# A hybrid S5 and attention layer on one core: x loaded first, parameters on GpSimdE's queue, C in longer runs, warm-up products ahead, another order of steps

## The chip, the cores and the metric

The kernel runs on one core of one Trainium2 chip, as one program. The metric is the device time in microseconds. TensorE multiplies and transposes into PSUM, VectorE and ScalarE work on SBUF and PSUM, GpSimdE works on SBUF, and loads are issued from the queues of SyncE, ScalarE and GpSimdE and carried by 16 DMA engines.

## The reference

One decoder layer on x of 256 tokens by 1024, all in float32. After an RMS norm, one projection (1024 to 2048) gives S5 inputs u and attention q, k, v. The S5 part has 32 groups of 16 channels with a diagonal complex state of 64 each; attention has 8 heads of 64 and, with 256 tokens, one causal block. Both outputs are normed, projected, added to x; then comes a SwiGLU layer of 2816.

```python
h = rmsnorm(x, g_pre_mix)
z = jnp.einsum('bsd,de->bse', h, w_in)
u, q, k, v = jnp.split(z, [D_SSM, D_SSM + D_ATTN, D_SSM + 2 * D_ATTN], axis=-1)
...
dt = jnp.exp(log_dt.astype(f32))[:, None]
mag = jnp.exp(a_re * dt)
ang = a_im * dt
lb_re = mag * jnp.cos(ang)
lb_im = mag * jnp.sin(ang)
...
bu_re = jnp.einsum('bsgh,gph->bsgp', uf, bb_re)
...
y = (jnp.einsum('bsgp,ghp->bsgh', st_re, c_re.astype(f32))
     - jnp.einsum('bsgp,ghp->bsgh', st_im, c_im.astype(f32))
     + d_skip.astype(f32) * uf)
...
mix = jnp.concatenate([rmsnorm(y_ssm, g_ssm_out), rmsnorm(y_attn, g_attn_out)], axis=-1)
x = x + rmsnorm(jnp.einsum('bse,ed->bsd', mix, w_out), g_post_mix)
h = rmsnorm(x, g_pre_ffn)
f = jax.nn.silu(jnp.einsum('bsd,df->bsf', h, w_gate)) * jnp.einsum('bsd,df->bsf', h, w_up)
x = x + rmsnorm(jnp.einsum('bsf,fd->bsd', f, w_down), g_post_ffn)
```

## The kernel before

The 256 tokens are two tiles of 128 partitions (`x_sb[0]`, `x_sb[1]`, four loads each). TensorE transposes x (L529), ScalarE and VectorE scale it by the gain into `xf`, and the four parts of the input projection multiply `xf` with weights that arrive in halves of pieces (`raw`, 512 KB each, L202): u (L564), then q and k (`qk_ps`, L873), then v (L899). All weight halves go out on SyncE's queue; a buffer must be free before its next load is issued, and the queue is served in order.

Beside that runs the S5 preparation. The parameters (`ldt`, `par_a`, `par_b`) are loaded, transposed on TensorE (L496, L497) and copied out of PSUM by VectorE into `par` (L498). From `par` VectorE computes the step by an exact exponential (`exp_a`, `exp_m`, `exp_k`, `exp_e`, `exp_r`, all 128x16), the eigenvalues `lam`, the coefficients `cf`, the phases `sph` and `pha`, and with the transposed B (`b_ps`) the input matrices `in_b` in two halves (task `bm`), which TensorE transposes (L812). With u transposed per token (`u_t`, L751) TensorE forms the states (`s_ps`, L966), VectorE scans them, and TensorE forms the outputs (L1007, L1010). C is transposed into `c_ps` (L730). The matrices `c_0`, `cm_r`, `cm_i` and `toep` are filled with zeros first (task `z`, L487), since only parts of them are written.

Behind the mixer come the gate, the norms and the output projection, then the feed-forward layer in 11 groups, where each weight is split into two float32r halves on ScalarE and VectorE (L123, L148) and each product becomes three (L261 to L263).

The order of the work is written out by hand in the table `ORDER`: each entry `name:n` takes n steps of a task, and on TensorE, VectorE and ScalarE every instruction is tied to the one before it. GpSimdE's and SyncE's instructions stand in the order in which the steps issue them. `wm` is a task of warm-up products of ones (L436) whose result is not used; `N_WARM` is their number. `ENG` moves single steps to another engine.

Of the kernel before, what the change touches and what calls it, by code (L numbers as in the profile page):

```python
# [41 lines left out]
bm1:1 bm0:1 u:1 ph:2 k:1 bm1:1 z:1 r:1 q:2 bm0:1 cv:1 k:1 ph:1 bm0:1 r:1 z:1 r:1 ph:1 k:2 q:1 bm1:1 ph:1 z:1 bm0:1 k:2
z:1 bm1:1 ct:1 k:2 ph:1 k:1 bm1:1 k:1 r:1 ph:2 r:2 bm0:1 k:1 bm1:1 r:2 cv:1 bm1:1 ct:3 bm1:1 r:1 q:1 bm0:2 k:1 q:2 r:1
k:2 u:1 cv:1 r:1 cv:1 bm0:1 k:1 q:1 r:3 ph:1 cf3:1 bm1:1 r:2 ut:1 cf3:1 ut:1 bm1:1 bm0:1 q:1 bm0:1 ut:1 bm1:1 q:1 ct:3
bm1:1 bm0:2 ct:3 bm1:1 q:1 ut:2 ct:1 q:1 k:1 ss1:1 k:1 q:2 om:2 to1:1 ss1:1 q:2 om:1 to1:1 bm0:1 to1:1 om:1 to1:1 om:1
k:1 ss1:1 to1:1 k:1 om:1 ss1:1 om:2 q:4 to1:1 k:1 ss1:1 ss0:2 ss1:1 ss0:1 ss1:1 ss0:1 k:1 ss0:1 k:3 om:1 to1:1 k:1
to0:2 q:1 to0:1 ss0:1 to0:1 q:1 ss0:1 k:1 ss1:1 q:1 k:1 ss1:1 q:3 om:1 to0:1 q:1 ss0:1 to0:1 ss1:1 to0:1 q:1 ss0:1 k:1
v:1 om:1 q:1 ss1:1 tf:1 k:1 ss0:1 q:1 ss1:1 tf:1 ss0:1 rr:1 ss0:1 rr:1 ss1:1 v:1 q:1 ss1:1 ss0:1 ss1:1 v:1 q:1 ss1:1
v:1 k:1 ss0:1 v:1 ss1:1 rr:1 k:1 ss0:1 v:2 q:1 v:1 rr:1 k:1 ss1:2 ss0:3 k:1 ss0:1 k:1 so1:1 so0:1 sc0:3 cv:1 sc0:3
so0:1 so1:1 sc0:5 lo:1 ex0:2 sc1:2 ex0:3 so1:1 ex0:1 sc1:2 sc2:1 sc1:1 sc2:3 sc1:2 sc2:1 cv:1 lo:1 ex0:1 sc2:2 ex1:1  # L50
ex0:1 ex1:1 ex2:1 so0:1 v:1 so1:1 ex0:1 so0:1 v:2 ex2:1 so0:1 ex1:2 ex2:1 v:1 ex2:1 so1:1 ex1:1 so0:2 so1:2 yt0:1 cv:1
# [1363 lines left out]
```

## Time and profile before

| what | value |
|---|---|
| time, median of 3 runs | 354.67 us (352.13 to 355.97) |
| the profiled execution's own time | 354.3 us |
| its span | 352.5 us |
| TensorE products busy | 328.3 us (93%) |
| VectorE busy | 219.0 us (62%) |
| ScalarE busy | 151.6 us (43%) |
| GpSimdE busy | 11.8 us (3%) |
| DMA | 53.46 MB, 152 GB/s on average |

Busy times are of one execution and of all stages together; the stages have different limits, so the stretches and the chain of work say more than the shares. TensorE's busy time holds time in which a product waits for its operands. In the rows PE is TensorE, PEld its weight load, DVE VectorE, ACT ScalarE, POOL GpSimdE and SP SyncE; a q behind the name is the queue from which loads are issued.

### The profile page before, as it was taken

How to read it: one execution, taken by the hardware profiler on the slowest of the kernel's cores; microseconds unless marked ns; L12 is line 12 of the kernel's file. 1: busy time of each engine (PE TensorE's matmuls, PEld its weight loads, DVE VectorE, ACT ScalarE, POOL GpSimd, SP SyncE). 2: the span in 40 equal slices, each digit the busy share in tenths (PEclk: the TensorE clock that was granted, in tenths of full speed). 3: DMA queues.
4: the chain of work that ended last, by engine and by line, in shares of the span. 5: the costliest groups of instructions: out<-in, count | busy, mean ns of one | idle time of the engine just before them, and what ended most of it. 6: DMA issues, size and time to landing. Idle time of an engine off the chain costs nothing.

```text
span 352.5 us, 5390 instructions
## 1 busy us (share of the span) xinstructions
PE 328.3 (93%) x2076; PEld 287.0 (81%) x2076; DVE 219.0 (62%) x472; ACT 151.6 (43%) x260; POOL 11.8 (3%) x23
## 2 busy tenths in 40 slices
PE   1899879999999999979999999999999999999990
PEld 1655669985977787779998899989999999999870
DVE  1489976469735999999644617783727273741054
ACT  1311277210688477563528108472626262631020
POOL 5100000040000000000000000000000000000001
PEclk9999989999999999999999999999999999999996
DMA  6899700010248328084753734988566564300022
GB/s 165 207 307 386 281 0 2 1 24 22 85 142 304 129 85 273 16 281 136 230 183 113 237 122 125 343 287 260 153 206 181 178 215 145 119 2 2 0 60 60
DMA packets 35785, 53.46 MB, mean 152 GB/s; under 512 B 3296, under 2 KB 25872, under 8 KB 35760
## 3 DMA queue, kind: packets, MB, share of 16 engines
...
HBM read 51.68 MB, written 1.05 MB: 150 GB/s over the span
## 4 chain that ended last, share of the span: by engine, by line
PE 75%; DVE 16%; DMA 5%; issue 2%; ACT 1%; DVEq 0%; ACTq 0%
PE gu L262 11%; PE gu L263 11%; PE gu L261 11%; PE qk_ps L873 6%; PE f_ps L261 6%; PE f_ps L262 6%; PE f_ps L263 6%; PE v_ps L899 4%; DVE w_lo L148 2%; DMA x<-in_x_dram 2%; PE yp L1010 2%; PE s_ps L966 2%; DMA par_b<-in_ssm_d_dram 1%; DVE rq L151 1%; DMA raw<-in_w_down_dram 1%
## 5 line engine op out<-in xcount | busy, mean ns | idle before, releaser
L148 DVE TENSOR_TENSOR w_lo<-raw,w_hi 128x1024 fp32r<-128x1024 f32 x76 | 91.6, 1222 | 37.9 <-ACT w_hi L123 37.6
L123 ACT CAST w_hi<-raw 128x1024 fp32r<-128x1024 f32 x73 | 75.2, 1048 | 55.8 <-PE f_ps L263 25.8
L261 PE MATMUL gu<-hx,w_hi 128*128 128x256 f32 x288 | 81.5, 283 | 0.0
L262 PE MATMUL gu<-hx,w_hi 128*128 128x256 f32 x288 | 81.4, 283 | 0.0
L263 PE MATMUL gu<-hx,w_lo 128*128 128x256 f32 x288 | 81.4, 283 | 0.0
L261 PEld LDWEIGHTS gu<-hx,w_hi 128*128 128x128 f32 x288 | 55.2, 192 | 0.5
L262 PEld LDWEIGHTS gu<-hx,w_hi 128*128 128x128 f32 x288 | 55.2, 192 | 0.5
L263 PEld LDWEIGHTS gu<-hx,w_lo 128*128 128x128 f32 x288 | 55.1, 192 | 0.1
L873 PE MATMUL qk_ps<-xf,raw 128*128 128x256 f32 x128 | 32.3, 390 | 0.0
L148 DVE TENSOR_TENSOR f<-f,gu 128x256 f32<-128x256 f32 x22 | 9.1, 420 | 33.1 <-ACT f L1257 27.1
L261 PE MATMUL f_ps<-w_hi,fh 128*128 128x512 f32 x72 | 28.2, 391 | 0.0
L262 PE MATMUL f_ps<-w_lo,fh 128*128 128x512 f32 x72 | 28.2, 391 | 0.0
L873 PEld LDWEIGHTS qk_ps<-xf,raw 128*128 128x128 f32 x128 | 23.7, 195 | 5.2 <-issue 2.9
L263 PE MATMUL f_ps<-w_hi,fl 128*128 128x512 f32 x72 | 27.2, 389 | 0.0
L1257 ACT ACTIVATE f<-gu 128x256 f32<-128x256 f32 x16 | 6.1, 381 | 32.4 <-PE gu L263 32.4
L261 PE MATMUL gu<-w_hi,hx 128*128 128x256 f32 x64 | 18.5, 290 | 0.0
L263 PE MATMUL gu<-w_hi,hx 128*128 128x256 f32 x64 | 18.2, 284 | 0.2 <-DVE hx L148 0.2
L262 PE MATMUL gu<-w_lo,hx 128*128 128x256 f32 x64 | 18.2, 285 | 0.1
L564 PE MATMUL u_ps<-raw,xf 128*128 128x512 f32 x32 | 17.0, 667 | 0.0
L263 PEld LDWEIGHTS f_ps<-w_hi,fl 128*128 128x128 f32 x72 | 13.5, 188 | 2.9
L261 PEld LDWEIGHTS f_ps<-w_hi,fh 128*128 128x128 f32 x72 | 13.6, 188 | 2.4
L262 PEld LDWEIGHTS f_ps<-w_lo,fh 128*128 128x128 f32 x72 | 13.6, 189 | 2.3
...
## 6 DMA issues: line engine op xcount, KB each, us to landing
raw<-in_w_gate_dram SPq DMA_DIRECT2D x22, 512.0 KB, 5.2
raw<-in_w_up_dram SPq DMA_DIRECT2D x22, 512.0 KB, 6.2
raw<-in_w_down_dram SPq DMA_DIRECT2D x22, 512.0 KB, 4.3
raw<-in_w_in_dram SPq DMA_DIRECT2D x13, 512.0 KB, 11.4
raw<-in_w_out_dram SPq DMA_DIRECT2D x8, 512.0 KB, 3.6
...
raw<-in_w_glu_dram SPq DMA_DIRECT2D x2, 512.0 KB
...
```

The lines of the kernel that those rows point to most:

```text
L123: e.copy(out=out, in_=in_) if e is nc.scalar else e.tensor_copy(out=out, in_=in_)
L148: return (eng or nc.vector).tensor_tensor(out=out, in0=a, in1=b, op=op)
L151: return nc.vector.scalar_tensor_tensor(out=out, in0=a, scalar=s, in1=b, op0=op0, op1=op1)
L261: nc.tensor.matmul(out=acc, lhsT=ah, rhs=bh, start=start, stop=False)
L262: nc.tensor.matmul(out=acc, lhsT=ah, rhs=bl, start=False, stop=False)
L263: nc.tensor.matmul(out=acc, lhsT=al, rhs=bh, start=False, stop=stop)
L564: nc.tensor.matmul(out=u_ps[t], lhsT=xf[k // 4][:, k % 4, P * t:P * (t + 1)], rhs=w[i], start=k == 0, stop=k == NK - 1)
L873: nc.tensor.matmul(out=o, lhsT=w[i][:, P * b:P * (b + 1)], rhs=xf[k // 4][:, k % 4], start=start, stop=stop)
L899: nc.tensor.matmul(out=v_ps[t], lhsT=xf[k // 4][:, k % 4, P * t:P * (t + 1)], rhs=w[i], start=k == 0, stop=k == NK - 1)
L966: nc.tensor.matmul(out=s[:, NC * i:NC * (i + 1)], lhsT=bm[:, HG * hf + i], rhs=u_t[:, :, HG * hf + i, :], start=(i == 0), stop=(i == HG - 1))
L1010: nc.tensor.matmul(out=o[:, 1:], lhsT=cm[:, gp].rearrange("p k g h -> p (k g h)"), rhs=xx[:, gp, 0:NC - 1], start=False, stop=(i == HG - 1 ...
L1257: nc.scalar.activation(out=f, in_=gu[:, 0:S], func=AF.Silu)
```

## The change

- The eight loads of x are the first on SyncE's and ScalarE's queues, four each. `gains` and the four parameter loads move to GpSimdE's queue; the activation that loads ScalarE's table (`warm`) comes behind the x loads.
- On SyncE's queue the gains of the mixer and b_glu (`g2`), and the three gain rows (`gr`, 512 KB each), move behind 13 weight halves; weight pieces are cut in two only for the first half, not for the first three.
- C is loaded by eight DMAs in runs of 1 KB (256 elements) instead of four in runs of 256 B, spread over 128 partitions; a copy on GpSimdE puts it in order, and TensorE transposes it in 4 instead of 16.
- `cm_r` and `cm_i` are filled on GpSimdE instead of VectorE. The fills of `gains` and `gains2` go; these are transposed from 8 rows.
- The warm-up products are 7 instead of 11, all ahead of everything else on TensorE.
- The table `ORDER` is new as a whole.

```diff
-N_WARM = 11
-N_FINE = 3
+N_WARM = 7
+N_FINE = 1
...
 ENG = {"fm11": "p", "ma00": "v", "ma01": "v", "ma10": "v", "ma11": "v", "ms01": "v", "na0": "v", "na1": "v",
-       "ns0": "v", "sqr00": "v", "sqrx1": "v", "xt1": "v", "z1": "v", "z2": "v"}
+       "ns0": "v", "sqr00": "v", "sqrx1": "v", "xt1": "v"}
...
-mk:1 x:1 lg:1 wm:1 x:1 mk:1 lp:2 wm:1 g2:1 x:1 lg:1 xt:3 z:1 xt:2 cv:1 xt:2 par:1 xt:2 par:1 cv:1 lb:1 u:1 la:1 dd:1
+x:3 mk:1 wm:6 lg:2 lp:2 z:1 wm:1 lw:1 lb:1 z:1 lp:1 lw:1 wm:1 z:3 xt:4 cv:1 xt:4 cv:1 par:1 xt:1 u:3 par:1 la:3 mk:1
...
-    nc.vector.memset(gains, 0.0)
-    nc.vector.memset(gains2, 0.0)
-    nc.scalar.activation(out=warm, in_=half_pi, func=AF.Sin)
...
     def load_gain():
-        nc.scalar.dma_start(out=gains[0:8, :], in_=rows(g_pre_mix))
+        nc.gpsimd.dma_start(out=gains, in_=rows(g_pre_mix))
...
     def load_parameters():
-        nc.scalar.dma_start(out=ldt, in_=ssm_log_dt[0].rearrange("(gp g) -> gp g", g=2))
-        nc.scalar.dma_start(out=par_a[0:GP, :], in_=ssm_a_re[0].rearrange(pair, g=2))
-        nc.scalar.dma_start(out=par_a[GP:32, :], in_=ssm_a_im[0].rearrange(pair, g=2))
-        nc.scalar.dma_start(out=par_b[GP:32, :],
+        nc.gpsimd.dma_start(out=ldt, in_=ssm_log_dt[0].rearrange("(gp g) -> gp g", g=2))
+        nc.gpsimd.dma_start(out=par_a[0:GP, :], in_=ssm_a_re[0].rearrange(pair, g=2))
+        nc.gpsimd.dma_start(out=par_a[GP:32, :], in_=ssm_a_im[0].rearrange(pair, g=2))
+        nc.gpsimd.dma_start(out=par_b[GP:32, :],
                           in_=ssm_d[0].rearrange(pair, g=2).unsqueeze(1).broadcast_to([GP, T4, 32]))
+        yield
+        nc.scalar.activation(out=warm, in_=half_pi, func=AF.Sin)
         yield
...
     def load_c():
         for row, m in ((0, ssm_c_re), (GP, ssm_c_im)):
-            for g in range(2):
-                nc.sync.dma_start(out=c_nat[row:row + GP].rearrange("r (h g p) -> r g h p", h=16, g=2)[:, g],
-                                  in_=m[0].rearrange("(gp g) h p -> g gp h p", g=2)[g])
+
+            for i in range(4):
+                nc.sync.dma_start(out=c_nat[32 * i + row:32 * i + row + GP, 0:512].rearrange("r (g x) -> r g x", g=2),
+                                  in_=m[0].rearrange("(gp g) h p -> gp g (h p)", g=2)[:, :, 256 * i:256 * (i + 1)])
+        yield
+        nc.gpsimd.tensor_copy(out=c_nat[:, DH:2 * DH].rearrange("r (h g p) -> r h g p", g=2, h=4),
+                              in_=c_nat[:, 0:DH].rearrange("r (g h p) -> r h g p", g=2, h=4))
         yield
...
-        for h in range(16):
-            nc.tensor.transpose(out=ps[:, 32 * h:32 * h + 32], in_=c_nat[:, P * h:P * (h + 1)], identity=id32)
-        yield
-        cp("c_sb", c_sb, ps.rearrange("p (h r g) -> p r g h", h=16, r=2))
+        for h in range(4):
+            nc.tensor.transpose(out=ps[:, P * h:P * (h + 1)], in_=c_nat[:, DH + P * h:DH + P * (h + 1)], identity=ident)
+        yield
+        cp("c_sb", c_sb.rearrange("p r g (i h) -> p (r g) i h", i=4), ps.rearrange("p (h i r) -> p r i h", h=4, i=4))
```

On GpSimdE, from the mask's fill to the sum of the skip diagonal into `toep`, there stood before (`c_110` is the zero matrix `c_0`, `diag_d` the skip diagonal):

```order
L1025 MEMSET mask 128x256
L487 MEMSET c_110 128x1024
L487 MEMSET toep 128x2048
L1028 AFFINE_SELECT mask<-mask 32x128 x4
L148 TENSOR_TENSOR diag_d<-ident,par 32x512
L945 MEMSET decay 128x16
L148 TENSOR_TENSOR toep<-toep,diag_d 32x16x32
```

and now, from the five loads on (the mask's fill stands right ahead of them, and `toep<-toep,diag_d` right behind):

```order
L445 DMA gains<-in_g_pre_mix_dram 8x128
L450 DMA ldt<-in_ssm_log_dt_dram 16x2
L451 DMA par_a<-in_ssm_a_re_dram 16x128
L452 DMA par_a<-in_ssm_a_im_dram 16x128
L453 DMA par_b<-in_ssm_d_dram 16x4x32
L489 MEMSET c_107 128x1024
L1031 AFFINE_SELECT mask<-mask 32x128 x4
L489 MEMSET cm_r 128x2048
L489 MEMSET cm_i 128x2048
L489 MEMSET toep 128x2048
L147 TENSOR_TENSOR diag_d<-ident,par 32x512
L475 COPY c_nat<-c_nat 128x512
```

The five loads stand ahead of the fills, two fills are new, and the copy of C is new behind them (the fill of `decay` stands between `diag_d` and that copy).

On TensorE, from the program's start to the first products of u and the transposes of b, before:

```order
L436 MATMUL wp<-ones 128x128 x2
L507 MATMUL gt<-ident,gains_84 128x32
L521 MATMUL gt<-ident,gains 128x32
L529 MATMUL tp<-ident,x_79 128x128 x8
L529 MATMUL tp<-ident,x_80 128x128 x8
L496 MATMUL gt<-ident,par_a 128x32
L497 MATMUL gt<-ident,par_b 128x32
L564 MATMUL u_ps<-raw,xf 128x512
L436 MATMUL wp<-ones 128x128
L720 MATMUL b_ps<-ident,b_nat 128x32 x16
L564 MATMUL u_ps<-raw,xf 128x512
```

and now, down to the first transpose of an input matrix:

```order
L432 MATMUL wp<-ones 128x128 x7
L524 MATMUL gt<-ident,gains 128x8
L532 MATMUL tp<-ident,x_79 128x128 x8
L532 MATMUL tp<-ident,x_80 128x128 x8
L498 MATMUL gt<-ident,par_a 128x32
L567 MATMUL u_ps<-raw,xf 128x512 x11
L723 MATMUL b_ps<-ident,b_nat 128x32 x16
L567 MATMUL u_ps<-raw,xf 128x512 x3
L876 MATMUL qk_ps<-xf,raw 128x256 x3
L567 MATMUL u_ps<-raw,xf 128x512 x2
L876 MATMUL qk_ps<-xf,raw 128x256 x15
L815 MATMUL tp<-ident,in_b 128x128 x4
```

The transpose of `gains2` has left the start, the warm-up products stand together, and 11 of the 16 products of u stand ahead of the transposes of b, where it was one.

On VectorE, in the middle of the input matrices, before:

```order
L148 TENSOR_TENSOR in_b<-b_ps,cf 128x4x4x32 x2
L148 TENSOR_TENSOR sph<-sph 128x256
L148 TENSOR_TENSOR pha<-sph 128x1024
L148 TENSOR_TENSOR bt<-b_ps,cf 128x4x4x32
L487 MEMSET cm_r 128x2048
L151 SCALAR_TENSOR_TENSOR rq<-ry,rv 128x1
L148 TENSOR_TENSOR bt<-b_ps,cf 128x4x4x32
L154 TENSOR_SCALAR phb<-pha 128x1024
L148 TENSOR_TENSOR in_b<-in_b,bt 128x512
L151 SCALAR_TENSOR_TENSOR ry<-rq,ry 128x1
L487 MEMSET cm_i 128x2048
L154 TENSOR_SCALAR ry<-ry 128x1
```

and now:

```order
L147 TENSOR_TENSOR in_b<-b_ps,cf 128x4x4x32 x2
L147 TENSOR_TENSOR sph<-sph 128x256
L147 TENSOR_TENSOR bt<-b_ps,cf 128x4x4x32
L147 TENSOR_TENSOR pha<-sph 128x1024
L150 SCALAR_TENSOR_TENSOR rq<-ry,rv 128x1
L153 TENSOR_SCALAR phb<-pha 128x1024
L150 SCALAR_TENSOR_TENSOR ry<-rq,ry 128x1
L147 TENSOR_TENSOR pha<-pha,phb 128x1024
L147 TENSOR_TENSOR bt<-b_ps,cf 128x4x4x32
L153 TENSOR_SCALAR ry<-ry 128x1
L147 TENSOR_TENSOR in_b<-in_b,bt 128x512 x2
```

The two fills are gone; the other instructions are the same and stand in nearly the same order.

## Rows read from the trace of the kernel before

**Rows 1.** Stretches: length, busy us of PE PEld DVE ACT POOL, PEclk, DMA, GB/s.

```profile
20.00:35.00 15.00, 15.00 (x46) 8.01 (x45) 13.59 (x67) 2.17 (x5) 0.12 (x1) 1.00 1.04 377
46.00:113.00 67.00, 67.00 (x403) 55.03 (x404) 43.41 (x97) 34.69 (x75) 4.29 (x4) 0.98 0.21 70
113.00:166.00 53.00, 49.63 (x301) 42.72 (x301) 50.98 (x132) 30.09 (x57) 0.00 (x0) 1.00 0.49 159
```

**Rows 2.** Chain that ended last, in order of time: start us, us, what.

```profile
3.21 5.60 DMA x<-in_x_dram
...
9.19 4.70 DMA par_b<-in_ssm_d_dram
...
14.34 0.24 DVE par L498
...
51.93 0.44 PE tp L812 x4
...
54.97 0.84 PE s_ps L966 x8
...
73.40 4.37 PE qk_ps L873 x20
...
103.25 6.06 PE v_ps L899 x14
```

**Rows 3.** Timeline, 0 to 45 us: start us, us, engine, line, operation, [idle before <-releaser].

```profile
1.09 1.22 PE L436 MATMUL wp<-ones 128*128 128x128 f32 x4 [1.09 <-DVE ones L284]
...
1.75 0.95 POOL L487 MEMSET c<- 128x1024 f32 x1
...
2.65 1.80 POOL L487 MEMSET toep<- 128x2048 f32 x1
...
4.40 1.36 POOL L1028 TENSOR_SCALAR_AFFINE_SELECT mask<-mask 32x128 f32<-32x128 f32 x4
...
9.34 3.67 PE L529 MATMUL tp<-ident,x 128*128 128x128 f32 x16
...
14.65 1.04 POOL L148 TENSOR_TENSOR diag_d<-ident,par 32x512 f32<-32x512 f32 x1 [8.88 <-DVE par L498]
14.81 0.92 DVE L154 TENSOR_SCALAR exp_m<-exp_a 128x16 f32<-128x16 f32 x1
...
15.97 0.17 DVE L151 SCALAR_TENSOR_TENSOR exp_r<-exp_k,exp_a 128x16 f32<-128x16 f32 x1
...
16.66 1.97 PE L720 MATMUL b_ps<-ident,b_nat 32*128 32x32 f32 x16
...
35.15 1.76 DVE L487 MEMSET cm_r<- 128x2048 f32 x1 [0.38 <-issue]
```

**Rows 4.** Stretch of 4 to 6 us, the columns of rows 1.

```profile
4.00:6.00 2.00, 0.00 (x0) 0.00 (x0) 0.00 (x0) 0.00 (x0) 1.62 (x5) 1.00 0.88 236
```

**Rows 5.** Timeline of GpSimdE, 70 to 90 us: the three loads of toep.

```profile
76.16 2.64 POOL L856 DMA_DIRECT2D toep<-toep  x3 [0.30 <-POOL toep L148]
```

**Rows 6.** Timeline of VectorE, 43 to 56 us: the second transpose of u.

```profile
51.77 0.71 DVE L751 STREAM_TRANSPOSE u_t<-u_n 128x512 f32<-128x512 f32 x1 [0.45 <-ACT u_n L128]
```

**Rows 7.** Timeline of TensorE, 40 to 50 us: the first input-matrix transposes.

```profile
45.91 1.09 PE L812 MATMUL tp<-ident,in_b 128*128 128x128 f32 x4 [2.91 <-DVE bt L148]
```

**Rows 8.** Stretch of 45.6 to 48.9 us, the columns of rows 1.

```profile
45.60:48.90 3.30, 2.99 (x11) 2.67 (x12) 3.06 (x15) 2.15 (x7) 0.00 (x0) 0.50 0.00 0
```

**Rows 9.** The line of the toep loads (L856): time from issue to landing.

```profile
DMA to landing us min/median/max: 2.4/2.8/3.9
```

**Rows 10.** Timeline, 339 to 352 us: GpSimdE beside VectorE.

```profile
344.50 1.26 POOL L148 TENSOR_TENSOR m<-m,g_row 128x512 f32<-128x512 f32 x1 [265.69 <-ACT m L1199]
344.60 1.17 DVE L151 SCALAR_TENSOR_TENSOR rq<-rq 128x1 f32<-128x1 f32 x1
345.80 0.16 DVE L151 SCALAR_TENSOR_TENSOR ry<-rq,ry 128x1 f32<-128x1 f32 x1
```

**Rows 11.** Page of the profile, its list of loads: weight halves, KB each, median us to landing.

```profile
raw<-in_w_in_dram SPq DMA_DIRECT2D x13, 512.0 KB, 11.4
```

More of the change, by code (lines that the diff above doesn't have):

```diff
@@ L42 @@
[L42 to L51, printed above, removed]
@@ new lines @@
+cv:1 po000:1 nm0:1 po001:1 cv:1 po001:2 po100:1 gl1:2 po100:1 cv:1 po101:1 po100:1 at1:1 cv:1 gl1:1 at1:2 po001:1 lo:1
+po100:1 lo:1 cv:1 po101:2 gl1:1 cv:1 nm1:1 po101:1 po100:1 nm1:1 at1:1 po101:1 nm1:1 at1:1 nm1:1 re0:2 nm1:1 at1:1
+nm1:2 at1:1 nm1:2 at1:1 nm1:1 re0:2 at1:1 re0:1 at1:1 re0:1 at1:2 po010:2 re0:1 nm1:1 re0:2 nm1:2 re0:1 nm1:1 po011:1
+re0:1 po010:1 nm1:1 cv:2 po010:1 po011:1 po010:1 po011:1 nm1:2 re0:1 nm1:1 cv:1 re0:1 nm1:2 po110:1 po011:1 re0:1
+po111:1 hx0:4 cv:1 po110:1 po111:1 lo:1 hx0:1 po110:1 lo:1 po011:1 hx0:1 po110:1 lo:1 po111:1 hx0:1 po111:2 hx0:1
@@ new lines @@
+po110:1 re1:2 hx0:1 re1:1 hx0:2 re1:1 hx0:1 re1:2 hx0:1 re1:1 hx0:1 lo:1 hx0:1 lo:1 re1:1 hx0:2 cv:1 hx0:1 cv:1 hx0:1
+ff00:1 cv:1 re1:1 ff00:1 re1:1 ff01:1 ff00:1 re1:1 cv:1 re1:1 ff01:1 lo:1 ff00:1 ff01:2 re1:1 ff00:1 ff01:1 re1:1
+ff01:1 ff00:1 hx1:1 ff01:1 hx1:6 ff01:1 hx1:2 ff00:1 lo:1 ff00:4 hx1:1 ff01:1 hx1:1 ff00:1 ff01:3 hx1:1 ff00:1 ff01:1
+ff00:1 ff01:1 hx1:2 ff01:1 hx1:1 lo:1 hx1:1 lo:1 ff00:2 hx1:3 ff10:1 ff11:1 ff01:1 ff10:1 ff11:1 ff01:1 lo:1 cv:1
+ff00:2 ff10:1 ff11:4 cv:1 ff10:2 ff11:1 lo:1 ff10:2 lo:1 ff11:1 ff10:1 ff11:1 ff01:1 ff10:2 ff11:1 cv:2 lo:1 ff11:3
@@ L70 @@
+ff10:1 lo:1 ff11:1 lo:1 ff10:1 lo:1 g2x:3 ff10:1 g2x:1 ff11:2 cv:1 ff11:1 ff01:1 ff10:3 ff11:1 ff00:1 lo:1 ff01:1
+ff00:1 g2x:1 ff10:1 g2x:1 ff10:1 cv:1 ff11:1 ff10:2 g2x:1 ff11:1 fp:1 g2x:1 fp:3 g2x:7 cv:1 lo:1 g2x:1 cv:2 g2x:1 cv:1
+g2x:2 lo:1 g2x:1 fp:2 g2x:1 cv:1 lo:1 fp:1 g2x:4 lo:2 g2x:2 cv:1 fp:2 lo:1 cv:1 g2x:2
 """
@@ L271, in hybrid_layer_kernel @@
     par_b = ssm.tile([32, P], F32, name="par_b")
-    gains = ssm.tile([32, P], F32, name="gains")
-    gains2 = ssm.tile([32, P], F32, name="gains2")
+    gains = ssm.tile([8, P], F32, name="gains")
+    gains2 = ssm.tile([8, P], F32, name="gains2")
     ldt = ssm.tile([GP, 2], F32, name="ldt")
     b_nat = ssm.tile([32, 2048], F32, name="b_nat", tag="k8", bufs=3)
-    c_nat = ssm.tile([32, 2048], F32, name="c_nat", tag="k8", bufs=3)
+    c_nat = ssm.tile([P, 2048], F32, name="c_nat", tag="k8", bufs=3)
     half_pi = const.tile([P, 1], F32, name="half_pi")
@@ L505, in mixer_gains @@
         nc.sync.dma_start(out=gains2[4:8, :], in_=rows(g_attn_out))
+        yield
         gt = bank("gt")
-        nc.tensor.transpose(out=gt[:, 0:32], in_=gains2, identity=id32)
+        nc.tensor.transpose(out=gt[:, 0:8], in_=gains2, identity=ident[0:8, 0:8])
         nc.vector.tensor_copy(out=par[:, 72:80], in_=gt[:, 0:8])
@@ L520, in transposed_x @@
         gt = bank("gt")
-        nc.tensor.transpose(out=gt[:, 0:32], in_=gains, identity=id32)
+        nc.tensor.transpose(out=gt[:, 0:8], in_=gains, identity=ident[0:8, 0:8])
         nc.vector.tensor_copy(out=gain_pre, in_=gt[:, 0:8])
```

38 lines of the change are left out of this document (17 added, 21 removed).

## The prediction

> **What bounds the kernel now.** I read the stretches first, then the chain that ended last, then the timeline of the first 20 us, and last the waits. TensorE is busy without a gap from 46 to 113 us and for 49.63 of the 53 us from 113 to 166, where VectorE is the fuller one, with 50.98 [rows 1]; the feed-forward groups behind that are TensorE's. So after 46 us there is next to no idle time to win; what can be won lies ahead of that, and whatever moves the start of the full stretch moves the end with it, as long as the work behind it keeps its order.
>
> The chain shows what sets that start [rows 2]. The last load of x lands at 8.81; the parameter load par_b is issued behind it on ScalarE's queue at 9.19 and takes 4.70 us; the parameters are copied out of PSUM at 14.34 (L498). From there the chain runs on VectorE through eigenvalues, coefficients and input matrices, with two memsets inside it, until TensorE can go on. The second transpose of u ends at 51.77 + 0.71 = 52.48 [rows 6], and the first state product s_ps starts at 54.97 [rows 2]. TensorE itself was late there: it had waited 2.91 us for VectorE [rows 7] and then worked on a granted clock of 0.50 (1.2 of its 2.4 GHz) from 45.6 to 48.9 [rows 8]. At the upper level four 128-wide transposes take 0.44 us [rows 2]; the four at 45.91 took 1.09 [rows 7].
>
> **The change part by part.** The sum is made on the profiled execution (354.3 us, which is 0.4 under the median of 354.67) and at one point: the start of s_ps, since from there on both kernels have almost the same work in the same order.
>
> x and the parameters. The eight loads of x are 1.05 MB. Before, the stretch from 4 to 6 us moved 236 GB/s [rows 4] with other loads among them; at that rate x takes 4.4 us and, if it starts to move at about 2 us, is there at 6.5 instead of 8.81. The seven warm-up products come first: two took 1.22 [rows 3], so seven take 4.3 and end at 5.4, before x is there; they cost nothing on the path. If the wait for x were gone, they would. The sixteen transposes of x took 3.67 [rows 3], half the rate of 0.44 for four [rows 2], although no lower clock is shown there; they end between 8.3 and 10.2, by the one rate or the other. The parameters now come by GpSimdE's queue. It is done with its mask memset at about 1.8, where its next fill began (1.75) [rows 3]; its three loads of toep took 2.64 us to issue, 0.88 each, and landed 2.4 to 3.9 us after issue [rows 5, 9]. Five of them end at 6.2, par_b is issued at about 5.3 and lands between 7.7 (2.4) and 10.0 (its own 4.70 of before). So the parameter copy comes at about 10.0 (8.9 to 11) instead of 14.34: **4.3 us earlier** (3.3 to 5.4).
>
> GpSimdE beside VectorE. The five loads push GpSimdE's other steps back, and the two memsets of cm_r and cm_i join them. By rows: loads to 6.2, c_0 0.95 to 7.2, four selects 1.36 to 8.5, then three fills of 128x2048 at 1.80 each to 10.3, 12.1 and 13.9, and diag_d 1.04 to 15.0 [rows 3]. That is just where the parameter chain now starts. Before, the scalar step exp_m on VectorE took 0.92 us where exp_r, of the same size, took 0.17, and ended when GpSimdE's diag_d did [rows 3]. A memset of GpSimdE beside such a step is in no row, so both bounds stand: free of it, exp_r starts 0.88 us after the parameter copy (1.63 in the rows less the 0.75 of that stall), at 10.9; held up by each instruction in turn, it starts at 14.0 to 15.0. Before it was 15.97. I take 14.5, near the held-up end, because exp_m is the only row in which such a step meets a longer GpSimdE instruction. So of the earlier copy **1.5 us** are left (1.0 to 5.1, or 6.2 with the copy at 8.9). If the copy came as late as before, the fills would be over, and this term would be near nought, not a loss.
>
> The Trainium skill, SBUF — State Buffer, section Who interferes with whom, says that VectorE and GpSimdE share one pair of ports as an exclusive lock, which tensor_scalar and copies can take and any GpSimdE instruction holds to its end. By that rule the fills hold VectorE's scalar steps up and the sum is the one above; without it the sum would be 3.6 us better. The trace agrees for an instruction that reads (0.92 beside 0.17) and has nothing on a fill.
>
> The two memsets leave VectorE: 1.76 us each, with 0.38 idle ahead of each [rows 3], 2 x 2.14 = **4.3 us** off the chain. Every other VectorE instruction between the parameter copy and the second transpose of u is there in both kernels, only in another order. What hides the fills from TensorE is that cm_r and cm_i are first written behind the second transpose of u, so 35 us later.
>
> C in runs of 1 KB: eight loads instead of four, and a 128x512 copy on GpSimdE at about 25 us, in the middle of the VectorE chain. The nearest rows: a 128x512 operation of GpSimdE took 1.26 us, and the VectorE step beside it 1.17, where its like took 0.16 [rows 10]. So a loss of 0 to 1.3; I take **-0.9**. The loads themselves stand behind eleven weight pieces; C is wanted only when the input matrices have been transposed.
>
> TensorE on the way. A product shows as two records. A qk record is 0.22 (4.37 for 20) and a 512-wide one 0.43 (6.06 for 14) [rows 2], so sixteen u products are 13.8 us, the eighteen qk products that now stand ahead of the first input-matrix transpose 7.9, and sixteen b transposes 2.0 [rows 3]. From 10.5 that ends at 34 to 36, when VectorE is ready at about 36. The weights ahead of them (x 1.05 MB, b and eight pieces, 5.5 MB in all) come at the 377 GB/s of 20 to 35 us [rows 1] well before they are wanted, because gains, b_glu and the 1.5 MB of gain rows no longer stand among them. So the first transpose should not come after a long idle stretch at the lower clock, and s_ps follows the transposes of u at once: of the 2.5 us between 52.48 and 54.97 I take **+2.0** back (0 to 2.5). VectorE also sat idle 0.45 us before the second transpose of u, for ScalarE [rows 6], and more before the first; with ScalarE's two u copies now right behind four bm_r copies I take **+0.6** (0 to 1.8). One qk product fewer is done by then: **-0.4**.
>
> Sum: 1.5 + 4.3 - 0.9 + 2.0 + 0.6 - 0.4 = 7.1 us. VectorE has 43.4 us of work in the 67 us that follow [rows 1], so it should not become the bound by being 2 us nearer to TensorE. At the end nothing is changed. The four warm-up products that are gone cost 0.6 us each only where TensorE was waiting anyway. 354.3 - 7.1 = 347.2, and 347.5 against the median; I say **347**.
>
> **The rivals.** First: the fills hold nobody up. Then the scalar chain keeps its 5.1 us, the sum is 10.7, and the time 343.6. For it: no row shows a memset stalling anybody. Against it: exp_m.
>
> Second: the gain is made and given back from 113 to 166, where VectorE has 2 us to spare in 53 and the glu and output weights come as buffers are set free [rows 1]; the new order there has two warm-up products less and other buffers. If half is lost, the time is 350.8. Against it: these waits hang on TensorE's own steps, which move too.
>
> Third, slower: the parameters get stuck. Small packets of GpSimdE's queue share the DMA engines with weight loads that take 11.4 us to land (median of 13 [rows 11]). The part of the sum that does not hang on their time is 5.6 us (4.3 - 0.9 + 2.0 + 0.6 - 0.4), so the change loses from the point at which the copy comes after 14.3 + 5.6 = 20 us, that is par_b landing 14 us after its issue; at 24 us the time is 358. With 11.4 us it is at 17.5, and the time still 352. Against it: par_b needed 4.70 among such loads.
>
> Fourth, the change doesn't do what it says: x lands no sooner, since the first weight pieces start as soon as the first x load has landed. Then the copy stays near 14, the fills are over by then, and the sum is 5.6 us: 348.7. It changes little, because early parameters meet the fills and late ones don't.
>
> **How the numbers follow.** About 1% (3.5 us) is what a measurement of this kernel can tell from no change. Chances: forecast 0.45 (345 to 349), no hold-up 0.25, nothing sooner 0.12, given back 0.13, slower 0.05. The ends of the terms are 1.0 + 4.3 - 1.3 + 0 + 0 - 0.4 = 3.6 (350.7) and 6.2 + 4.3 + 0 + 2.5 + 1.8 - 0.4 = 14.4 (339.9); the top end hardly comes in all terms at once, so the range is 341.5 to 351.5, which leaves out the slower case and a part of the given-back one. Faster by over 1% (under 351.1): all of the first three and half of the fourth, 0.86, less a little for terms that fail together, 0.84; within 1% 0.11; slower 0.05.
>
> **What would show it.** In the timeline of the changed kernel: x transposes from about 6.5, parameter copy near 10, then VectorE's exp_a to exp_e at 1 to 2 us each, ending with GpSimdE's fills; no memset in the chain; the first input-matrix transpose near 37, s_ps near 47.5; behind it the same distances as before. If the exp steps take 0.17 the first rival holds. Wrong it would be if TensorE had waits of several us after s_ps that were not there before, or if par_b landed after 15 us.

## The result and the profile after

The changed kernel takes 343.81 us, the median of four runs, against 355.09 for the kernel before: a ratio of 0.9708 with a 95% interval of 0.9666 to 0.975, so 2.9% faster; the ratio is worked out from the single runs and is not the quotient of the two medians, which is 0.968. One run of an experiment below (e7) took 656.82 us and is in no ratio; what held it up was not recorded. The forecast was 347.0 with a range of 341.5 to 351.5. The time lies in the range and nearly on the figure of the first rival (343.6), though that rival's mechanism is not what the trace shows.

The changed kernel's trace is of its slowest run, 344.63 us; the other three took 343.80 to 343.82. The two traces (354.3 and 344.63) are thus 9.7 us apart and the medians 11.3, and what is read from the traces below accounts for the smaller of the two.

The timeline of the changed kernel, 0 to 14.5 us, with the columns of rows 3, answers to rows 3:

```profile
1.09 3.36 PE L432 MATMUL wp<-ones 128*128 128x128 f32 x14 [1.09 <-DVE ones L283]
...
3.93 0.54 POOL L453 DMA_DIRECT2D par_b<-in_ssm_d_dram  x1
...
5.36 1.38 POOL L1031 TENSOR_SCALAR_AFFINE_SELECT mask<-mask 32x128 f32<-32x128 f32 x4
...
7.46 0.24 PE L524 MATMUL gt<-ident,gains 8*128 8x8 f32 x1 [3.01 <-DMA gains<-in_g_pre_mix_dram]
...
8.03 3.65 PE L532 MATMUL tp<-ident,x 128*128 128x128 f32 x16 [0.34 <-DMA b_nat<-in_ssm_b_im_dram]
...
10.28 1.80 POOL L489 MEMSET toep<- 128x2048 f32 x1
...
11.35 0.81 DVE L495 COPY par_b<-ldt 16x128 f32<-16x128 f32 x1
...
12.21 0.25 PE L499 MATMUL gt<-ident,par_b 32*128 32x32 f32 x1 [0.29 <-DVE par_b L495]
...
12.50 0.22 DVE L500 COPY par<-gt 128x64 f32<-128x64 f32 x1 [0.34 <-PE gt L499]
...
12.88 1.04 POOL L147 TENSOR_TENSOR diag_d<-ident,par 32x512 f32<-32x512 f32 x1 [0.80 <-DVE par L500]
...
12.97 0.99 DVE L153 TENSOR_SCALAR exp_m<-exp_a 128x16 f32<-128x16 f32 x1
...
14.20 0.18 DVE L150 SCALAR_TENSOR_TENSOR exp_r<-exp_k,exp_a 128x16 f32<-128x16 f32 x1
```

Here the reader sees three things. TensorE had done its warm-ups at 4.45, stood idle for 3.01 us until the gains were there, and then took 3.65 us for the transposes of x, the half rate again. The copy of ldt took 0.81 us and ended at 12.16, when the fill of toep ended (12.08); TensorE's transpose of `par_b` (L499) waited for it. So the parameter copy came at 12.50, not at 10.0, and exp_r at 14.20, so 1.77 us sooner than before.

Why the parameters were not the limit, from the list of loads of 0 to 12 us (queue, KB each, median us to landing):

```profile
x<-in_x_dram SPq DMA_DIRECT2D x4, 128.0 KB, 4.5
...
par_b<-in_ssm_d_dram POOLq DMA_DIRECT2D x1, 8.0 KB, 4.9
```

par_b landed at 3.93 + 4.9 = 8.8 us and its issue took 0.54 us, where I had 0.88 by [rows 5]. It was there 2.5 us before the copy of ldt, so the transposes of x and the fill set the date. The shorter issues also ended the fills sooner: the toep fill was over at 12.08 and not at 13.9.

From there on, the timeline of TensorE, 33 to 46 us, answers to [rows 7] and to the s_ps of [rows 2]:

```profile
36.08 0.60 PE L815 MATMUL tp<-ident,in_b 128*128 128x128 f32 x4
...
43.50 0.60 PE L876 MATMUL qk_ps<-xf,raw 128*128 128x256 f32 x2
44.06 0.43 PE L969 MATMUL s_ps<-u_t,bm_r 128*128 128x64 f32 x2
```

and the groups of VectorE, 14.2 to 44.1 us (busy us, mean ns, idle before), to [rows 6]:

```profile
L754 DVE STREAM_TRANSPOSE u_t<-u_n 128x512 f32<-128x512 f32 x2 | 1.3, 684 | 0.0
```

For comparison the kernel before, the same two views (timeline of TensorE, 53 to 56 us; groups of VectorE, 15.97 to 54.8 us):

```profile
53.07 1.89 PE L873 MATMUL qk_ps<-xf,raw 128*128 128x256 f32 x8
54.80 0.33 PE L966 MATMUL s_ps<-u_t,bm_r 128*128 128x64 f32 x2
```

```profile
L751 DVE STREAM_TRANSPOSE u_t<-u_n 128x512 f32<-128x512 f32 x2 | 1.4, 711 | 1.8 <-ACT u_n L128 1.8
```

So s_ps came 10.74 us sooner (54.80 to 44.06). That is 1.77 by exp_r, 4.28 by the two fills (2 x (1.76 + 0.38), [rows 3]), 1.8 by VectorE's waits for ScalarE ahead of u_t (1.35 ahead of the first, 0.45 ahead of the second), and 2.26 by TensorE, which now starts s_ps 0.06 us behind the second u_t and not 2.32; 0.63 are small gaps. The parts are differences of two single traces. TensorE waited nowhere for long: 1.1 us at c_ps in the whole of 30 to 45 us.

The stretches with the columns of rows 1 answer to [rows 1]; the second and third are shifted by 9.3 us with the work, and the last is a stretch of low clock:

```profile
20.00:35.00 15.00, 15.00 (x62) 10.31 (x61) 14.12 (x64) 1.58 (x2) 0.73 (x2) 1.00 0.86 287
36.70:103.70 67.00, 65.70 (x400) 52.89 (x400) 47.41 (x105) 36.53 (x79) 4.18 (x4) 1.00 0.22 74
103.70:156.70 53.00, 50.55 (x304) 44.05 (x303) 49.19 (x131) 30.57 (x58) 0.00 (x0) 0.97 0.54 180
142.00:145.40 3.40, 3.40 (x19) 3.40 (x18) 3.06 (x5) 1.87 (x3) 0.00 (x0) 0.50 0.82 299
```

TensorE stays full (65.70 of 67 us and 50.55 of 53), so the gain is carried on: the output projection ends 10.37 us sooner (149.60 to 139.23), the last product 9.84 sooner (343.14 to 333.30). The largest loss behind s_ps is 0.95 us at the sixteen transposes behind the output projection, of which 0.4 is won again later. Timeline of TensorE, before and then after:

```profile
151.47 2.05 PE L359 MATMUL tp<-dg,xg 128*128 128x128 f32 x16 [1.87 <-DVE dg L154]
```

```profile
141.08 3.00 PE L355 MATMUL tp<-dg,xg 128*128 128x128 f32 x16 [1.85 <-DVE dg L153]
```

They fell into a stretch of granted clock 0.50 (1.2 of 2.4 GHz). The kernel before had none there; its own such stretch was at 45.6 to 48.9 us [rows 8].

### The profile page after: what moved, and what is told of

Read it like the earlier page. It is cut to its first block, busy times and chain, and to the rows that moved or that the text cites. A ratio compares the mean times of both kernels' runs of the same rounds, so it can differ in the third digit from the quotient of the medians.

```text
span 342.6 us, 5373 instructions
## 1 busy us (share of the span) xinstructions
PE 324.8 (95%) x2056; PEld 284.7 (83%) x2056; DVE 216.3 (63%) x468; ACT 151.9 (44%) x260; POOL 18.5 (5%) x31
## 3 DMA queue, kind: packets, MB, share of 16 engines
q10 hardware_dynamic: 576, 1.05, 1.3%
HBM read 51.68 MB, written 1.05 MB: 154 GB/s over the span
## 4 chain that ended last, share of the span: by engine, by line
PE 75%; DVE 16%; ACT 3%; issue 2%; DMA 1%; SPq 1%; DVEq 0%; ACTq 0%
PE gu L260 12%; PE gu L262 12%; PE gu L261 12%; PE f_ps L260 6%; PE f_ps L261 6%; PE f_ps L262 6%; PE qk_ps L876 5%; PE v_ps L902 4%; DVE w_lo L147 2%; PE yp L1013 2%; PE s_ps L969 2%; DMA x<-in_x_dram 1%; DVE rq L150 1%; DVE in_b L147 1%; PE yp L1010 1%
## 5 line engine op out<-in xcount | busy, mean ns | idle before, releaser
L876 PE MATMUL qk_ps<-xf,raw 128*128 128x256 f32 x128 | 31.2, 383 | 0.0
L147 POOL TENSOR_TENSOR m<-m,g_row 128x512 f32<-128x512 f32 x1 | 1.3, 1261 | 266.2 <-ACT m L1202 266.2
```

The source lines that it names most:

```text
L147: return (eng or nc.vector).tensor_tensor(out=out, in0=a, in1=b, op=op)
L876: nc.tensor.matmul(out=o, lhsT=w[i][:, P * b:P * (b + 1)], rhs=xf[k // 4][:, k % 4], start=start, stop=stop)
```

## The experiments

All times are medians; ratios are to the kernel before, run on the same chip beside them. s_ps, exp_r and the last product are from the profiled execution.

| kernel | median us | ratio (95%) | exp_r | s_ps | last product ends |
|---|---|---|---|---|---|
| before | 355.09 | 1 | 15.97 | 54.80 | 343.14 |
| after | 343.81 | 0.9708 (0.9666 to 0.975) | 14.20 | 44.06 | 333.30 |
| e1_fills_pool | 349.99 | 0.9876 (0.9827 to 0.9926) | 14.92 | 48.26 | 337.71 |
| e2_old_order | 348.92 | 0.983 (0.979 to 0.987) | 14.29 | 49.25 | 338.20 |
| e3_warm13 | 344.64 | 0.9703 (0.9671 to 0.9736) | 14.23 | 44.09 | 333.34 |
| e4_fills_dve | 343.72 | 0.9681 (0.9652 to 0.9711) | 13.93 | 43.97 | 332.52 |
| e5_loads_early | 351.29 | 0.9956 (0.9923 to 0.999) | 14.29 | 51.58 | 340.16 |
| e6_fills_mid | 348.28 | 0.9895 (0.988 to 0.991) | 13.71 | 47.77 | 337.30 |
| e7_params_act | 343.32 | 0.9694 (0.965 to 0.9738) | 13.71 | 43.58 | 332.11 |
| e8_warm21_fills_dve | 343.27 | 0.9688 (0.9653 to 0.9724) | 13.11 | 43.33 | 331.76 |
| e9_warm21 | 344.76 | 0.9727 (0.969 to 0.9764) | 14.21 | 44.21 | 332.71 |
| e10_no_warm | 344.27 | 0.972 (0.9685 to 0.9756) | 14.26 | 44.28 | 332.90 |
| e11_warm18_params_act | 343.03 | 0.9703 (0.9667 to 0.9739) | 13.39 | 43.24 | 331.76 |
| e12_c_runs | 345.36 | 0.9767 (0.9733 to 0.9801) | 14.30 | 44.71 | 334.33 |

The kernel before took 352.31 beside e5 and e6 and 353.76 to 355.09 beside the others, so ratios of two groups can be a per cent apart for equal times; times of this table are compared with after's 343.81, and differences under a microsecond between kernels timed in different groups say little.

The theory at the start was the sum of the prediction; the rivals were that the fills do it all, or that the order does it all.

**e1_fills_pool.** The kernel before with its two fills on GpSimdE.

```diff
-       "ns0": "v", "sqr00": "v", "sqrx1": "v", "xt1": "v", "z1": "v", "z2": "v"}
+       "ns0": "v", "sqr00": "v", "sqrx1": "v", "xt1": "v"}
```

> The kernel before with one part of the change: cm_r and cm_i filled on GpSimdE, where they stand at 4.5 to 8 us, long before VectorE's chain begins. Theory (the fills are 4.3 us of the chain that leads to the first input-matrix transpose, and the rest of the gain is the order and the earlier parameters): TensorE has finished its products ahead of that transpose at 43.0, so it can start at 43.0 instead of 45.9 and should not fall to the lower clock; s_ps 3 to 4.5 us earlier, time 350 to 352. Rival (the fills were hidden, and the gain of the change comes from loading x first): 354 to 355.

349.99, at the lower edge of the theory's range; the rival is out. s_ps came 6.54 us sooner, more than the 3 to 4.5 expected, but 1.05 of that stands at exp_r already, where this edit moves nothing; the parameters were there sooner in this execution. The chain that ended last in it, in order of time (start us, us, what), shows what came up behind VectorE:

```profile
33.17 4.12 PE qk_ps L873 x18
...
38.41 2.35 PE qk_ps L873 x10
...
42.36 3.02 PE qk_ps L873 x14
...
46.69 1.73 PE qk_ps L873 x8
```

From 33 us on it is TensorE's own work that stands ahead of s_ps, at a granted clock of 1.00, and s_ps starts 2.12 us behind the second u_t. Moving the fills alone makes TensorE the bound. Of VectorE's two waits ahead of u_t only the second is left (timeline of VectorE, 38 to 56 us):

```profile
45.43 0.71 DVE L751 STREAM_TRANSPOSE u_t<-u_n 128x512 f32<-128x512 f32 x1 [0.45 <-ACT u_n L128]
```

**e2_old_order.** The changed kernel with the old table of steps (the steps that were split or are new fitted in).

```diff
-N_WARM = 7
+N_WARM = 11
...
-x:3 mk:1 wm:6 lg:2 lp:2 z:1 wm:1 lw:1 lb:1 z:1 lp:1 lw:1 wm:1 z:3 xt:4 ...
+mk:1 x:1 lg:1 wm:1 x:1 mk:1 lp:3 wm:1 g2:1 x:1 lg:1 xt:3 z:1 ...
```

> All code of the change (x and parameter loads, C in runs of 1 KB, fills on GpSimdE), but the order table, warm-up products and their number of the kernel before. Theory (of the 10.7 us at s_ps, 1.8 are the earlier parameter copy, 4.3 the fills, and 4.6 the order: TensorE no longer late, ScalarE's u copies sooner): 348 to 350. Rival (the order is worth nothing, the loads and fills everything): 343.5 to 345.

348.92, in the theory's range: exp_r came as early as in the changed kernel (14.29), and 5 us were lost behind it. Again TensorE had no gap from 35.1 us on and started s_ps 2.12 us behind the second u_t; it had waited for weights just before (timeline of TensorE, 33 to 36.5 us):

```profile
35.14 1.56 PE L877 MATMUL qk_ps<-xf,raw 128*128 128x256 f32 x6 [0.61 <-DMA raw<-in_w_in_dram]
```

The theory by now: the order's part is one of loads. The next kernel puts nothing back but these; C keeps its eight loads, where the kernel before had four.

**e5_loads_early.** The changed kernel with four loading steps back in their old places on SyncE's queue (b_glu and the mixer gains, C, and the gain rows).

```diff
-x:3 mk:1 wm:6 lg:2 lp:2 ...
+x:3 mk:1 g2:1 wm:6 lg:2 lp:2 ...
-... par:1 xt:1 u:3 par:1 la:3 ... cv:1 xs:1 cv:1 la:2 u:1 ag:1
+... par:1 xt:1 lc:1 u:3 par:1 la:3 ... cv:1 xs:1 gr:1 cv:1 la:2 u:1 ag:1
-... bt:1 u:1 gr:1 ... q:1 u:1 lc:3 u:1 ... ph:1 g2:1 bm1:1
+... bt:1 u:1 ... q:1 u:1 lc:2 u:1 ... ph:1 bm1:1
```

> The changed kernel, with only the loads put back in the order list: b_glu and the mixer gains right behind x, C behind the third piece of weights, the three gain rows behind two pieces more; every step that computes stays where the change has it. Theory: what the new order brings is that the weight pieces come first, so TensorE has done its u products by 30 us. With the loads back it waits for weights and works without a gap from 33 to 35 us on, the first s_ps comes at 47 to 49.5 us instead of 44.06, and the time is 347 to 349.5 us. Rival: the order of the computing steps does it (ScalarE's copies, fewer products ahead of s_ps). Then s_ps stays at 44 to 45.3 and the time at 343.5 to 345.

351.29, s_ps at 51.58: the rival is out, and the effect is larger than the theory said. TensorE, 24 to 46 us (timeline):

```profile
28.62 0.67 PE L876 MATMUL qk_ps<-xf,raw 128*128 128x256 f32 x2 [0.75 <-DMA raw<-in_w_in_dram]
34.04 2.04 PE L876 MATMUL qk_ps<-xf,raw 128*128 128x256 f32 x4 [4.75 <-DMA raw<-in_w_in_dram]
35.88 2.87 PE L567 MATMUL u_ps<-raw,xf 128*128 128x512 f32 x4
38.59 6.64 PE L876 MATMUL qk_ps<-xf,raw 128*128 128x256 f32 x30
```

and stretches (columns of rows 1):

```profile
30.00:35.00 5.00, 0.96 (x2) 0.84 (x3) 5.00 (x10) 0.00 (x0) 0.00 (x0) 0.60 1.05 387
35.00:40.00 5.00, 5.00 (x14) 3.11 (x13) 4.96 (x12) 3.77 (x5) 0.00 (x0) 0.71 1.05 385
```

It waits 5.5 us for weights, and after that wait works on a granted clock of 0.50 until 37.9. That second loss, about 2 us, is what the range left out: the four records of u took 2.87 us, where they took 1.88 in the changed kernel. The loads' issues say how the queue got there, SyncE's timeline of this kernel, then of after and of the kernel before (issue start us, us):

```profile
10.59 0.44 SPq L201 DMA_DIRECT2D raw<-in_w_in_dram  x1
11.07 2.53 SPq L472 DMA_DIRECT2D c_nat<-in_ssm_c_re_dram  x4
13.65 2.49 SPq L472 DMA_DIRECT2D c_nat<-in_ssm_c_im_dram  x4
16.19 1.09 SPq L201 DMA_DIRECT2D raw<-in_w_in_dram  x2
```

```profile
8.27 8.28 SPq L201 DMA_DIRECT2D raw<-in_w_in_dram  x11
17.11 4.62 SPq L472 DMA_DIRECT2D c_nat<-in_ssm_c_re_dram  x4
```

```profile
13.90 0.83 SPq L473 DMA_DIRECT2D c_nat<-in_ssm_c_re_dram  x2
14.86 0.86 SPq L473 DMA_DIRECT2D c_nat<-in_ssm_c_im_dram  x2
```

By 16.6 us twelve weight halves had been issued in the changed kernel (the first in two loads) and fewer than four here, since the eight loads of C hold the queue for 5.1 us and move little. The four loads of C in the kernel before held it for 1.8 us. So the 7.5 us are the price of these places for the new steps and the eight loads together, and not the share that the order of loads has in the gain: e2, with the same loads in the old places and the old steps, lost 5.1. What the new steps would cost with the four old loads was not run.

**e6_fills_mid.** The changed kernel with the two fills on VectorE, in the middle of its chain.

```diff
-    blank = [c_0, cm_r, cm_i, toep]
+    blank = [c_0, toep, cm_r, cm_i]
...
-       "ns0": "v", "sqr00": "v", "sqrx1": "v", "xt1": "v"}
+       "ns0": "v", "sqr00": "v", "sqrx1": "v", "xt1": "v", "z2": "v", "z3": "v"}
...
-... lw:1 wm:1 z:3 xt:4 ... bm0:1 ph:1 r:1 u:1 ph:1 q:2
+... lw:1 wm:1 xt:4 ... bm0:1 z:1 ph:1 r:1 u:1 ph:1 z:2 q:2
```

> The changed kernel with the two fills of cm_r and cm_i back on VectorE and back in the middle of its chain, behind bt and behind phb. Theory: in the new order VectorE's chain alone sets s_ps, so both fills cost their full 3.5 to 4.3 us: s_ps at 47.6 to 48.4 us and the time 347.2 to 348.2 us. Rival: TensorE is close behind VectorE in the new order too, as it was in the old order with the fills gone, and hides more than half of them: s_ps at 44.5 to 46 and the time under 346.

348.28, 0.08 over the theory's range; s_ps is 3.71 later, inside it. Since exp_r came 0.49 sooner without these fills on GpSimdE, the way from exp_r to s_ps is 4.20 longer, near the 4.28 counted for the two fills. TensorE now waits for VectorE (timeline, 31 to 41 us), so in the new order VectorE's chain is the bound again and the fills cost what they take:

```profile
39.52 1.11 PE L815 MATMUL tp<-ident,in_b 128*128 128x128 f32 x4 [3.62 <-DVE in_b L147]
```

**e12_c_runs.** The changed kernel with C loaded and transposed as before, in the new place.

```diff
-            for i in range(4):
-                nc.sync.dma_start(out=c_nat[32 * i + row:32 * i + row + GP, 0:512] ...
-        nc.gpsimd.tensor_copy(out=c_nat[:, DH:2 * DH] ...
+            for g in range(2):
+                nc.sync.dma_start(out=c_nat[row:row + GP].rearrange("r (h g p) -> r g h p", h=16, g=2)[:, g], ...
...
-        for h in range(4):
+        for h in range(16):
```

> The changed kernel with C loaded as before: four loads in short runs into 32 partitions, sixteen transposes instead of four, no copy on GpSimdE; in the same place of the order. Theory: this part of the change is worth nothing that can be measured. The GpSimdE copy held no VectorE step, the four transposes save 0.5 us of TensorE where it waits for VectorE anyway, and four loads stand in place of eight on SP's queue: s_ps at 43.8 to 44.8 us, time 343.4 to 344.6. Rival: the short runs hold back the weight pieces behind them, TensorE becomes late for the input matrices, and the time is 345.5 us or more.

345.36: over the theory's range and just under the rival's. C's part is a gain of about 1 to 1.5 us by this comparison, which is under the 1% that can be told; I had booked a loss of 0.9. The four transposes became these sixteen (timeline of TensorE, 36 to 46 us):

```profile
40.49 1.15 PE L729 MATMUL c_ps<-ident,c_nat 32*128 32x32 f32 x16 [0.87 <-issue]
```

1.15 against 0.63 us, ahead of the last input-matrix transposes. From there TensorE has no gap to s_ps in either kernel, so the 0.52 is on the path: the second u_t ends 0.11 later than in the changed kernel (44.11), and s_ps starts 0.60 us behind it where it was 0.06. The expectation had taken TensorE to wait for VectorE there. s_ps is 0.65 later, the output projection ends 1.01 later (140.24 against 139.23). Where the other 0.4 to 0.9 come from was not separated.

**e4_fills_dve.** The changed kernel with the two fills on VectorE at 2 to 6 us, where it is idle.

```diff
-       "ns0": "v", "sqr00": "v", "sqrx1": "v", "xt1": "v"}
+       "ns0": "v", "sqr00": "v", "sqrx1": "v", "xt1": "v", "z1": "v", "z2": "v"}
```

> The changed kernel with cm_r and cm_i filled on VectorE, in the new order at about 2 to 6 us where VectorE is idle, so that GpSimdE's last fill ends near 8.6 instead of 12.1. Theory (the fill of toep stretched the copy of ldt from 0.20 to 0.81 us, and TensorE's last parameter transpose waits for it): 0.6 us less, 343.0 to 343.5, with the ldt copy at 0.2. Rival (that copy is slow for another reason): it stays at 0.8, time 343.8.

343.72, no different, though the copy of ldt did what the theory said: in the timeline of VectorE it takes a quarter of its time, the toep fill being over at 8.62. Of the 0.27 us won at exp_r, 0.09 are left at s_ps.

```profile
11.51 0.20 DVE L495 COPY par_b<-ldt 16x128 f32<-16x128 f32 x1
```

**e3_warm13** (13 warm-up products instead of 7), **e10_no_warm** (none), **e9_warm21** (21) and **e8_warm21_fills_dve** (21, with the fills as in e4).

```diff
-N_WARM = 7
+N_WARM = 21
...
-x:3 mk:1 wm:6 lg:2 lp:2 ...
+x:3 mk:1 wm:20 lg:2 lp:2 ...
```

> The changed kernel with 13 instead of 7 warm-up products, which end about when x is there. Theory (the sixteen x transposes run at half rate because TensorE has been idle from 4.5 to 7.4 us, and GpSimdE's fill of toep holds up VectorE's copies and scalar steps until 12.1): the transposes take 1.8 instead of 3.65 us, the parameter copy comes 1 to 1.5 us earlier, but the exp steps then meet the fill and diag_d; 343.0 to 344. Rival (fills hold nobody up): 342 to 342.5.

> The changed kernel with no warm-up product at all. Theory: the granted clock of TensorE comes up later than 12.3 us and some of the u products run at half rate, but TensorE has time to spare until 36 us: the first in_b transpose stays near 36.1 us and the time is 343.6 to 344.3 us. Rival: TensorE becomes late for the input matrices: s_ps at 45 us or later and 344.7 us or more.

> The changed kernel with 21 warm-up products, fills left on GpSimdE. Theory: if a fill holds VectorE's small steps, the copy of ldt still ends with the toep fill at 12.1 us however soon TensorE has done its transposes, and the parameter copy stays at 12.4 to 12.6 us, the time at 343.5 to 344.1 us. Rival: the fill does not hold it; then the copy comes at 10.6 to 11.3 us and the time is that of the same kernel with the fills on VectorE, 342.2 to 343.1 us.

> The changed kernel with 21 warm-up products ahead of all else, so that TensorE is at work until x is there, and the fills of cm_r and cm_i on VectorE at 2 to 6 us, where it is idle. Theory: TensorE goes into the sixteen transposes of x at its upper level, they take 1.8 to 2.3 us instead of 3.65, and with no fill beside the parameter steps the parameter copy comes at 10.6 to 11.3 us, s_ps at 42.5 to 43.4 and the time is 342.2 to 343.1 us. Rival: the transposes stay at half rate, or the products hold back the gains' transpose: copy at 12.2 or later and 343.6 us or more.

e3: 344.64, 0.6 over the theory's range; 13 products end at 6.2 us, TensorE then waits 1.3 us for the gains, and the transposes of x took 3.41 us and not the expected 1.8. e10: 344.27, in the theory's range; the 22 records of u behind the transposes took 10.69 us against 9.71 in the changed kernel, s_ps is 0.22 later, and it is as fast within what can be told. The seven warm-up products of the change bring nothing measurable. With 21, TensorE works until x is there, and the transposes of x take 1.97 us. Timeline of e9 and then of e8:

```profile
11.21 0.95 DVE L495 COPY par_b<-ldt 16x128 f32<-16x128 f32 x1
```

```profile
8.61 1.97 PE L532 MATMUL tp<-ident,x 128*128 128x128 f32 x16
...
10.86 0.20 DVE L495 COPY par_b<-ldt 16x128 f32<-16x128 f32 x1
...
13.11 0.17 DVE L150 SCALAR_TENSOR_TENSOR exp_r<-exp_k,exp_a 128x16 f32<-128x16 f32 x1
```

The two differ in the fills alone: with them on GpSimdE the copy of ldt still ends with the toep fill (12.16 against 12.09), and exp_r stays at 14.21; without them exp_r comes 1.10 us sooner. So a fill does hold VectorE's small steps up. The other kernels agree: in all seven with this fill beside it (after, e2, e3, e5, e9, e10, e12) the copy ended 0.07 to 0.08 us behind the fill, whether it had begun at 11.21 or at 11.87, and in the five without (e4, e6, e7, e8, e11) it took 0.20. e9's time of 344.76 is 0.7 over its range, and I have no row for that. e8's is 343.27, a little over its range, as is its parameter copy (11.40); 0.73 at s_ps became half a microsecond.

**e7_params_act.** Gains and parameter loads on ScalarE's queue, behind x.

```diff
-        nc.gpsimd.dma_start(out=gains, in_=rows(g_pre_mix))
+        nc.scalar.dma_start(out=gains, in_=rows(g_pre_mix))
...
-        nc.gpsimd.dma_start(out=ldt, in_=ssm_log_dt[0].rearrange("(gp g) -> gp g", g=2))
+        nc.scalar.dma_start(out=ldt, in_=ssm_log_dt[0].rearrange("(gp g) -> gp g", g=2))
```

(and the other three likewise)

> The changed kernel with gains and the four parameter loads on ScalarE's queue, right behind its four loads of x, instead of on GpSimdE's. Theory: x and TensorE set the parameter copy, not the queue; GpSimdE's fills come 2.7 us sooner, so the toep fill is over by 9.5 us and the copy of ldt takes 0.20 us and not 0.81; parameter copy at 12.2 us, time 343.2 to 343.9 us. Rival: these loads land later than on GpSimdE's queue, as par_b did before (4.70 us behind x), and the parameter copy comes at 13.5 us or later: 345 us or more.

343.32, in the theory's range; par_b is issued at 8.2 us and is still in time, the fills are over by 7.9, and the copy of ldt takes 0.20. GpSimdE's queue was not needed; half a microsecond is at the edge of what the runs tell.

**e11_warm18_params_act.** e7 with 18 warm-up products.

> The changed kernel with both small edits that each gave about half a microsecond: gains and parameter loads on ScalarE's queue behind x, and 18 warm-up products (21 lasted to 8.45 us, x is there at 8.0). Fills stay on GpSimdE, where they now end by 8 us. Theory: the two gains add, since the one takes away the fill beside the copy of ldt and the other halves the transposes of x: transposes of x 8.0 to 10.0 us, parameter copy at 10.8 to 11.3, s_ps at 42.7 to 43.3 and the time 342.6 to 343.2 us. Rival: both reach the same bound, TensorE and ScalarE between 30 and 44 us, and the time is 343.2 to 343.6 us as for each alone.

343.03, the lowest time of all and in the theory's range, but the two gains hardly add: exp_r is at 13.39 and s_ps at 43.24, 0.09 before e8's. Its parameter copy came at 11.76, later than the 10.8 to 11.3 expected. It beats both kernels, the changed one by 0.8 us, under the 1% that can be told.

## Why the prediction was right, step by step

The forecast's mechanism held: an earlier start of s_ps, carried to the end by a full TensorE. Its sum was 7.1 us and measured 10.74 at s_ps, so it was a third short, and several terms were right for other reasons than the ones given.

- **x at 6.5 us** was wrong. The last issue of x ended at 2.6 us, x took 4.5 to 4.7 to land (medians of the two queues), and the transposes began at 8.03. I had divided bytes by the rate of 4 to 6 us [rows 4] and left the time from issue to landing out.
- **Parameter copy at 10.0**: measured 12.50, 1.84 and not 4.3 us sooner. The landing was sized about rightly, the issues too long: the five loads were issued by 4.47 us and not 6.2. x, the half-rate transposes and the fill set the date. The bounds (8.9 to 11) missed it.
- **Fills hold VectorE's scalar steps; 1.5 us left**: measured 1.77 at exp_r, of which up to a microsecond may be chance, since e1, whose way to exp_r is that of the kernel before, has it at 14.92 and not 15.97. The hold-up struck one step ahead, at the copy of ldt (0.81 against 0.20), and exp_m again stood beside diag_d (0.99). e9 against e8 shows it. The size was right partly by luck, since errors cancelled: the parameters came 2.5 us later than forecast, the fills ended 1.8 us sooner, and so only one fill was met. exp_a and exp_k took 0.17, which the prediction had named as the sign of its first rival; with the fills over by 12.08 that sign could not tell. The Trainium skill's rule (SBUF — State Buffer, Who interferes with whom), an exclusive lock that a copy can take and a GpSimdE instruction holds to its end, agrees with 0.81 beside the fill and 0.20 without it, and now for an instruction that only writes.
- **Two fills off VectorE, 4.3**: e6 gives 3.71 at s_ps, 4.20 from exp_r on, and 4.5 in time. Right, with the new order. With the old order it is TensorE that would have met s_ps, so the term needed the next one.
- **TensorE no longer late, +2.0**: measured 2.26, but not by the low clock alone, which the prediction had named: e1 and e2 run at 1.00 there without a gap, and s_ps still starts 2.12 us behind the second u_t. In them and in the kernel before, 13 qk products stand on TensorE between the first input-matrix transposes and s_ps, in the changed kernel 10; two of the other three now stand ahead of these transposes, where TensorE arrives at 36.08 without a gap, near the forecast of 34 to 36, and one behind s_ps. And the sentence under it, that weights come well before they are wanted because gains, b_glu and gain rows no longer stand among them, carried more than 2.0: e5 takes that away and loses 7.5 us of the 11, though with eight loads of C, which hold the queue for 5.1 us, in place of four that held it for 1.8. I had named C's eight loads only as standing behind eleven weight pieces, and not what they cost ahead of them.
- **ScalarE's copies, +0.6**: measured 1.8, the upper bound of the range given. The waits ahead of both transposes of u are gone, not only the second's 0.45. It is only in part ScalarE's: before, ScalarE itself had waited 1.02 us for TensorE's late transposes (bm_r at 48.74). With the fills moved and the old order (e1, e2) the 1.35 ahead of the first is gone and the 0.45 is still there, so only the 0.45 is the order's.
- **C, -0.9**: nothing of it. The GpSimdE copy took 0.61 us at 29.3, and no VectorE step beside it was long. e12 gives a gain of about 1 us, half of it in TensorE's transposes, which the prediction did not count.
- **One qk product fewer, -0.4**: not visible by itself.

What moved the time under the forecast is thus ScalarE (1.2 more), C (0.9), small gaps (0.63), 0.3 each for exp_r and TensorE and the 0.4 of the qk product that was not seen, less 0.9 given back: 2.8 us, so 344.4 for the traced run, which took 344.63. That the median lies 0.8 lower is outside this sum.

Two smaller slips change little: seven warm-up products took 3.36 us and not 4.3, and the chances of the first four cases add up to 0.885 and not 0.86 (all of three and half of the fourth).

Of the rivals, the first has the right number (10.7 at s_ps) by luck and the wrong reason: e9 against e8 and the copy of ldt show the hold-up. The second, the gain given back between 113 and 166 us, is out but for the 0.9 us named above. The third did not occur, as par_b landed after 4.9 us. The fourth was true in part, the transposes of x began 1.3 and not near 3 us sooner, and it cost little for the reason given.
